# A decoder block in one program: the stream that prepares the feed-forward operands, its steps, its engines and the order behind it

## The chip, the core and the metric

One core of a Trainium2 chip runs the whole kernel as one program. The metric is the device time of one execution in microseconds (us), the median of several runs. A profiled execution of the same program gives, for each engine, when each instruction ran. The engines are TensorE (PE, with weight loads as PEld), VectorE (DVE), ScalarE (ACT), GpSimd (POOL) and SyncE (SP), which here only issues DMAs. Each engine works through its own queue in order; semaphores tie the queues together. SBUF is the on-chip memory of 128 partitions, PSUM the memory that PE writes, and the DRAM tensors lie in HBM.

## What is computed

One decoder layer on a sequence of 2048 tokens of width 1024, in float32. A mixer sub-layer (windowed attention beside an mLSTM, gated and merged, then `w_out`) gives `x`, and a SwiGLU feed-forward network (FFN) of width 2816 follows:

```python
x = x + gate_m[:, None, :] * rms_norm(mix, g_post_mix[l])

h2 = modulate(rms_norm(x, g_pre_ffn[l]), shift_f, scale_f)
ff = (jax.nn.silu(h2 @ w_ffn_gate[l]) * (h2 @ w_ffn_up[l])) @ w_ffn_down[l]
x = x + gate_f[:, None, :] * rms_norm(ff, g_post_ffn[l])
```

The change concerns `h2`, the first operand of the FFN's matmuls.

## The kernel before, in words

**Tiles and numbers.** Every float32 matmul is done as three matmuls of split numbers: a value is cut into a high part (ACT copies it to the reduced format, `split_unit`, L1112) and a low part (DVE subtracts, L1113), and high x high, high x low and low x high are added up in PSUM. Each such matmul has 512 columns.

**Mixer.** Four blocks of 512 tokens (`block(b)`) run one after the other. A block ends with the mLSTM's branch projection (`branch_tiles` on `w_bm`, 96 matmuls) and the output projection with the residual (`residual_out`, 2 halves of 96 matmuls). The residual's tail, for each of four token tiles: ACT squares the sum (L523), DVE multiplies by the gain (L525), POOL raises to the power -1/2 (L473), DVE and POOL add to rows of `x` that were loaded by L552 (L537, L540), SP writes the new `x1` (L541), ACT squares again (L542), DVE adds the sums (L543), and POOL makes `rx`, the reciprocal norm for the next sub-layer. These use the buffers `tx` (6 of them); most other scratch of the mixer is `tm` (9).

**FFN.** Tokens are taken in two halves of 1024 (`b2`). For each half, `gate_up(b2)` makes gate and up projections and `down(b2)` the down projection. Each product of 2x2 blocks is done with seven block products instead of eight (a Winograd-Strassen form). The seven right operands are called, in the order of the products, 11, 21, T2, T4, T1, T3, 22 (`PROD`); 11, 12, 21, 22 are the quarters of the transposed `h2` and the T's are differences of them. The seven left operands are quarters of the weights and their sums: 11, 12, S2, 22, S1, S3, S4. S1 and S2 are made by DVE (L1254, L1255) into buffers `w` that `unit()` takes from the FFN's pool.

**The stream that is changed.** `h_combine(b2, ...)` makes the right operands, in four steps `k` (a quarter of the width's 128-column groups each). A step loads four pieces of `x1` by four DMAs (L1193), multiplies each by `rx` (L1197), transposes them on PE (L1204, L209) into PSUM, scales and shifts them to 11, 12, 21, 22 (ACT L1209, DVE L1207), makes T1, T2, T3, T4 by subtractions (L1214 to L1222), and splits all seven. For the first half of tokens it runs inside the last mixer block: its pieces lie in `tm` buffers, its products and differences are done by POOL (`G` in `HC_FROM_MIXER`), and since SBUF is full at that point, two operands are **parked**: T3 and 22 are written to the DRAM tensor `hc_d` (L1224) and read back by `rest_of_hc` (L1237), which makes their low parts (L1240) and 22's high part (L1239) once the mixer's buffers are given up. For the second half it runs inside `down(0)`, all on DVE, with pieces in `big` buffers.

**What sets the order.** The kernel is written out by Python in one pass. PE's work is written as it comes, and a planned clock `now` is advanced by each matmul. Streams are generators: `yield d` means "go on when `now` has advanced by `d` ns". `spawn(gen, delay)` starts one, `tick()` steps those that are due, and `finish` steps a stream to its end whatever the clock says. In the mixer `tick` runs after each group of matmuls. In `run2`, which drives the FFN, it runs only in parts marked `weave`, that is, in those of the seven down products that accumulate into one PSUM group (first, third, fifth and seventh, 11 parts each). The written order is the priority; when the program is built, each engine's queue is laid down from it by what is then expected to be ready.

`run2` itself loads weights ahead and prepares up to four parts (gate and up) or two (down) ahead: this is `advance()`, called before and after each part. Between mixer and FFN stands `open_ffn`: it closes the mixer's pools, opens the FFN's pool over the same memory (each tile waits for those it overlays), loads the gain `gg_f` there (L1497), and calls `rest_of_hc`. The FFN's first `advance()` came after that.

Of the kernel before, what the change touches and what calls it, by code (L numbers as in the profile page):

```python
# [19 lines left out]
P = 128  # L20
# [47 lines left out]
def decoder_block(ctx: ExitStack, tc: tile.TileContext, a: dict, out: bass.AP, dbg=None):  # L68
# [582 lines left out]
    def block(b):  # L651
# [393 lines left out]
        def stage5():  # L1045
            finish(R["ml"])
            finish(R["outs"])
            if b + 1 == NBLK:
                finish(R_ada)
                open_hc()  # L1050
                R["hc"] = spawn(h_combine(0, *HC_FROM_MIXER), 8000.0)
            for i in range(2):
                A.activation(R["gm", i], R["gm", i], AF.Sigmoid)

# [67 lines left out]
    def run2(items):  # L1122
        items = list(items)
        parts = [p for p in items if isinstance(p, Part)]
        raws = []
        for p in parts:
            if p.raw not in raws:
                raws.append(p.raw)
        nload = nprep = done = 0
        made = {}  # L1130

        def advance():
            nonlocal nload, nprep
            while True:
                alive = sum(1 for r in raws[max(0, nload - 3):nload] if r.left)
                if nload < len(raws) and alive < 2:
                    raws[nload].tile = raws[nload].load()
                    nload += 1
                    continue
                if nprep < len(parts) and nprep < done + parts[nprep].ahead and parts[nprep].raw.tile is not None:  # L1140
                    p = parts[nprep]
                    made[nprep] = p.prep()
                    p.raw.left -= 1
                    nprep += 1
                    continue
                return

        for it in items:
            if not isinstance(it, Part):
                it()  # L1150
                continue
            advance()
            for _ in it.mms(made.pop(done)):
                if it.weave:
                    tick()
            done += 1
            advance()
# [21 lines left out]
    def four(t):  # L1179
        return [t[:, i * 4:(i + 1) * 4, :] for i in range(4)]  # L1180


    HC_FROM_MIXER = (lambda: [tm([P, 4, P]) for _ in range(4)], lambda: tm([P, TB]), lambda: tm([P, TB]), G)

    def h_combine(b2, rows, quarters, sums, eng):


        wait = b2 == 0
        for k in range(4):
            xk = rows()  # L1190
            for j, (half, i) in enumerate(((0, 0), (0, 1), (1, 0), (1, 1))):
                c0 = (k + 4 * half) * P
                nc.sync.dma_start(xk[j], x1[b2 * 2 + i][:, c0:c0 + P].rearrange("(t p) c -> p t c", p=P))  # L1193
            yield 12000.0
            for j in range(4):
                t0 = b2 * 8 + (j % 2) * 4
                eng.tensor_tensor(xk[j], xk[j], rx[:, t0:t0 + 4].unsqueeze(2).to_broadcast([P, 4, P]), op=ALU.mult)  # L1197
            yield 4000.0
            v = {}
            for j, (half, i) in enumerate(((0, 0), (0, 1), (1, 0), (1, 1))):  # L1200
                kk = k + 4 * half
                ps = mix_tile()
                for t in range(4):
                    transpose(ps[:, t * P:(t + 1) * P], xk[j][:, t, :])  # L1204
                q = quarters()
                if wait and i:
                    V.tensor_scalar(q, ps, s2[:, kk:kk + 1], sh2[:, kk:kk + 1], op0=ALU.mult, op1=ALU.add)  # L1207
                else:
                    A.activation(q, ps, AF.Identity, scale=s2[:, kk:kk + 1], bias=sh2[:, kk:kk + 1])  # L1209
                v[f"{half + 1}{i + 1}"] = q  # L1210
                if i:
                    yield 1500.0
            v["T1"] = sums()
            eng.tensor_tensor(v["T1"], v["12"], v["11"], op=ALU.subtract)  # L1214
            v["T2"] = sums()
            eng.tensor_tensor(v["T2"], v["22"], v["T1"], op=ALU.subtract)
            eng.tensor_tensor(v["12"], v["22"], v["12"], op=ALU.subtract)
            v["T3"] = v.pop("12")
            for name in NAMES:
                if name == "T4":  # L1220
                    v["T4"] = sums()
                    eng.tensor_tensor(v["T4"], v["21"], v["T2"], op=ALU.subtract)  # L1222
                if wait and name in ("T3", "22"):
                    nc.sync.dma_start(hc_d[:, ("T3", "22").index(name), k, :], v[name])  # L1224
# [8 lines left out]
    def rest_of_hc():  # L1233
        for i, name in enumerate(("T3", "22")):
            for k in range(4):
                u = unit()
                nc.sync.dma_start(u, hc_d[:, i, k, :])  # L1237
                if name == "22":
                    A.copy(hc_part("22", 0)[:, k, :], u)  # L1239
                V.tensor_tensor(hc_part(name, 1)[:, k, :], u, HC[name][0][:, k, :].bitcast(F32), op=ALU.subtract)  # L1240
# [158 lines left out]
    def down(b2):  # L1399
# [71 lines left out]
        if not last:  # L1471
            def next_h():
                q4 = []

                def quarters():
                    if not q4:
                        t = big([4, TB])
                        q4.extend(t[:, i, :] for i in range(4))
                    return q4.pop()

                F["hp"] = spawn(h_combine(b2 + 1, lambda: four(big([16, P])), quarters, unit, V))

            yield next_h
        for i in range(7):
# [8 lines left out]
    def open_ffn():  # L1493
        p1.close()
        F["pool"] = ctx.enter_context(tc.tile_pool(name="fpool", bufs=1, reuse_waits="tile"))
        F["gg"] = F["pool"].tile([P, D], F32, name="gg_f")
        nc.sync.dma_start(F["gg"], gg_f_d)  # L1497
        rest_of_hc()

    def program():  # L1500
        for i, ch in enumerate(ADA):
# [7 lines left out]
    open_ffn()  # L1509

    def program2():
        for b2 in range(NB2):
            yield from gate_up(b2)
            yield from down(b2)
# [28 lines left out]
```

## Time and profile before

| | us |
|---|---|
| median of 3 runs | 2827.76 |
| lowest and highest run | 2825.27, 2830.12 |
| the profiled execution, its own time | 2826.42 |
| its span, first to last instruction | 2824.6 |

The page of the profile lists the busy time of each engine, the span in 40 slices, and the costliest groups of instructions. A row of a timeline has start, duration, engine, line, operation, what it writes and reads (buffer numbers left out), its shape and a count when neighbours are merged; in brackets stands the idle time of the engine just before it and who ended it. Rows with SPq are DMA issues. A view by form gives minimum, median and maximum duration in ns and the first and last start. A matmul is in flight longer than the next one waits, so the cost of one is the distance from start to start.

### The profile page before, as it was taken

Reading aid. Unit: us, or ns where it says so; the run is one execution under the profiler, and the core shown is the slowest. Engines: PE = TensorE matmul, PEld = TensorE weight load, DVE = VectorE, ACT = ScalarE, POOL = GpSimd, SP = SyncE. Lnnn points to the kernel's source line nnn. Section 1 sums busy time; section 2 is a strip of 40 time slices with the busy share of each in tenths; the row PEclk is TensorE's granted clock in tenths of the full one; section 3 lists DMA queues with packets and bytes.
Section 4 is the critical chain, followed back from the end, with each engine's and each line's share of the span. In section 5 each row is a group of like instructions: output and inputs, shape, how many; then the busy total and the mean of one; then the engine's idle time right before and its main releaser. Section 6 shows DMA issues by size and latency. Waiting matters only on the chain.

```text
span 2824.6 us, 35115 instructions
## 1 busy us (share of the span) xinstructions
PE 2720.0 (96%) x12654; PEld 2204.8 (78%) x12654; DVE 1935.0 (69%) x3756; ACT 1226.6 (43%) x2269; POOL 283.2 (10%) x287
## 2 busy tenths in 40 slices
PE   6999999999999999999987999999998999999997
PEld 4778887788877887778876788887776888888886
DVE  7768666586575876757677966766757666666556
ACT  4543365434644336543343333334554333333443
POOL 3100120012200012101272000000000000000000
PEclk8999999999999999999998999999999999999999
DMA  7234252243522425323357932335557233234557
GB/s 228 90 108 106 95 188 93 82 116 107 181 87 82 133 81 182 100 81 97 94 182 244 308 109 97 112 110 170 194 179 241 95 112 105 97 108 140 181 197 242
DMA packets 274773, 392.14 MB, mean 139 GB/s; under 512 B 18580, under 2 KB 175896, under 8 KB 274600
## 3 DMA queue, kind: packets, MB, share of 16 engines
q1 hardware_dynamic: 274600, 389.91, 43.0%
q8 instruction: 99, 1.62, 0.2%
q14 instruction: 74, 0.61, 0.1%
HBM read 318.52 MB, written 71.34 MB: 138 GB/s over the span
## 4 chain that ended last, share of the span: by engine, by line
PE 81%; DVE 8%; DMA 7%; ACT 2%; issue 1%; POOL 1%; SPq 0%; DVEq 0%; POOLq 0%; ACTq 0%
PE acc L204 57%; PE mix L204 22%; PE mix L209 2%; DVE hl L1113 1%; DMA tx<-in_x_dram 1%; DMA big<-in_w_ffn_down_dram 1%; DMA ws_d<-big 1%; DMA tx<-in_w_ada_dram 1%; DVE tm L424 1%; DMA raw<-in_w_ffn_down_dram 1%; ACT hl L1112 1%; DMA x<-tx 0%; DMA raw<-as_d 0%; DVE wlo L260 0%; DMA big<-in_x_dram 0%
## 5 line engine op out<-in xcount | busy, mean ns | idle before, releaser
L1112 ACT CAST hl<-raw 128x512 fp32r<-128x512 f32 x528 | 314.7, 621 | 444.3 <-PE mix L204 189.4
L1113 DVE TENSOR_TENSOR hl<-raw,hl 128x512 fp32r<-128x512 f32 x528 | 352.5, 688 | 191.0 <-ACT hl L1112 188.8
L259 ACT CAST whi<-raw 128x1024 fp32r<-128x1024 f32 (+1 forms) x208 | 212.1, 1020 | 476.0 <-PE acc L204 417.5
L260 DVE TENSOR_TENSOR wlo<-raw,whi 128x1024 fp32r<-128x1024 f32 (+1 forms) x208 | 255.4, 1228 | 173.1 <-ACT whi L259 172.1
L204 PE MATMUL acc<-hhi,wlo 128*128 128x512 f32 x896 | 354.5, 396 | 0.0
L204 PE MATMUL acc<-hlo,whi 128*128 128x512 f32 x896 | 352.1, 393 | 0.0
L204 PE MATMUL acc<-hhi,whi 128*128 128x512 f32 x896 | 352.0, 393 | 0.0
L204 PE MATMUL acc<-hl,hl 128*128 128x512 f32 x1056 | 252.4, 397 | 18.4 <-DVE hl L1113 12.1
L204 PE MATMUL acc<-big,hl 128*128 128x512 f32 x1056 | 253.7, 389 | 0.0
L204 PEld LDWEIGHTS acc<-hl,hl 128*128 128x128 f32 x1056 | 198.0, 190 | 68.6 <-DVE hl L1113 18.7
L204 PEld LDWEIGHTS acc<-big,hl 128*128 128x128 f32 x1056 | 198.2, 188 | 41.2
L204 PEld LDWEIGHTS acc<-hlo,whi 128*128 128x128 f32 x896 | 168.3, 188 | 41.0 <-issue 6.5
L204 PEld LDWEIGHTS acc<-hhi,whi 128*128 128x128 f32 x896 | 168.4, 188 | 39.5 <-issue 6.5
L204 PE MATMUL mix<-big,hl 128*128 128x512 f32 x704 | 197.4, 391 | 1.4 <-DVE hl L1113 1.4
L204 PEld LDWEIGHTS acc<-hhi,wlo 128*128 128x128 f32 x896 | 168.3, 188 | 38.5 <-issue 4.1
L204 PE MATMUL mix<-hl,hl 128*128 128x512 f32 x792 | 182.1, 390 | 1.3 <-ACT hl L1112 1.2
L204 PEld LDWEIGHTS mix<-hl,hl 128*128 128x128 f32 x792 | 148.0, 188 | 34.9 <-ACT hl L1112 4.2
L473 POOL TENSOR_TENSOR rs<-ms,nhalf 128x1 f32<-128x1 f32 (+1 forms) x40 | 29.2, 733 | 1436.0 <-DVE ms L470 1409.7
L204 PE MATMUL acc<-whi,big 128*128 128x512 f32 x512 | 165.9, 396 | 0.0
L204 PE MATMUL acc<-big,whi 128*128 128x512 f32 x512 | 157.9, 393 | 0.0
L204 PEld LDWEIGHTS mix<-big,hl 128*128 128x128 f32 x704 | 132.2, 188 | 30.3 <-DVE hl L1113 2.2
L204 PE MATMUL acc<-wlo,hhi 128*128 128x512 f32 (+1 forms) x384 | 139.7, 368 | 3.3 <-DVE wlo L260 2.5
(317 smaller groups left out, 5014.6 us busy)
## 6 DMA issues: line engine op xcount, KB each, us to landing
raw<-in_w_in_dram SPq DMA_DIRECT2D x76, 1024.0 KB, 5.4
as_d<-w SPq DMA_DIRECT2D x154, 256.0 KB, 2.1
raw<-as_d SPq DMA_DIRECT2D x70, 512.0 KB, 3.8
raw<-in_w_ffn_gate_dram SPq DMA_DIRECT2D x22, 1024.0 KB, 6.8
raw<-in_w_ffn_up_dram SPq DMA_DIRECT2D x22, 1024.0 KB, 5.4
raw<-ws_d SPq DMA_DIRECT2D x40, 512.0 KB, 4.7
tx<-in_w_ada_dram SPq DMA_DIRECT2D x64, 256.0 KB, 4.2
raw<-in_w_out_dram SPq DMA_DIRECT2D x16, 1024.0 KB, 5.0
```

What stands on the lines that cost most here:

```text
L204: T.matmul(o, lhsT=lhsT, rhs=rhs, start=start, stop=stop, skip_group_check=resumed)
L209: T.transpose(o, i, ident[:k, :k])
L259: A.copy(hv, src)
L260: eng.tensor_tensor(lv, src, hv.bitcast(F32), op=ALU.subtract)
L424: V.scalar_tensor_tensor(acc, raw[:, k, :], c_, acc, op0=ALU.mult, op1=ALU.add)
L473: G.tensor_tensor(r[:, :n], ms[:, :n], nhalf[:, :n], op=ALU.pow)
L1112: A.copy(v(hi), src)
L1113: V.tensor_tensor(v(lo), src, v(hi).bitcast(F32), op=ALU.subtract)
```

## The change

Four things change.

1. `h_combine` for the first half starts 3000 ns of planned time after its spawn (before: 8000), its first rows are followed by 8000 (before: 12000 in each step), and the products by 3000 (before: 4000). The rows of step `k + 1` are loaded inside step `k`, after its transposes and ahead of its differences.
2. The one engine becomes a pair. The first stream gets (POOL, DVE): products alternate, T1 and T2 go to POOL, T3 and T4 to DVE. The second stream gets (DVE, DVE). T1, T2 and T4 of the first stream now lie in `tx` buffers, before in `tm`.
3. `run2` calls `advance()` once before it looks at its first item.
4. `rest_of_hc` is no longer called in `open_ffn`, but is the first item of the FFN's program, so it is written after that first `advance()`.

The steps of `h_combine` are the same for the second half, so its spacing changes too.

```diff
-                R["hc"] = spawn(h_combine(0, *HC_FROM_MIXER), 8000.0)
+                R["hc"] = spawn(h_combine(0, *HC_FROM_MIXER), 3000.0)
...
+        advance()
         for it in items:
             if not isinstance(it, Part):
                 it()
...
-    HC_FROM_MIXER = (lambda: [tm([P, 4, P]) for _ in range(4)], lambda: tm([P, TB]), lambda: tm([P, TB]), G)
+    HC_FROM_MIXER = (lambda: [tm([P, 4, P]) for _ in range(4)], lambda: tm([P, TB]), lambda: tx([P, TB]), (G, V))
 
-    def h_combine(b2, rows, quarters, sums, eng):
+    def h_combine(b2, rows, quarters, sums, engs):
 
         wait = b2 == 0
-        for k in range(4):
+        QUADS = ((0, 0), (0, 1), (1, 0), (1, 1))
+
+        def load(k):
             xk = rows()
-            for j, (half, i) in enumerate(((0, 0), (0, 1), (1, 0), (1, 1))):
+            for j, (half, i) in enumerate(QUADS):
                 c0 = (k + 4 * half) * P
                 nc.sync.dma_start(xk[j], x1[b2 * 2 + i][:, c0:c0 + P].rearrange("(t p) c -> p t c", p=P))
-            yield 12000.0
+            return xk
+
+        xn = load(0)
+        yield 8000.0
+        for k in range(4):
+            xk = xn
             for j in range(4):
                 t0 = b2 * 8 + (j % 2) * 4
-                eng.tensor_tensor(xk[j], xk[j], rx[:, t0:t0 + 4].unsqueeze(2).to_broadcast([P, 4, P]), op=ALU.mult)
-            yield 4000.0
+                engs[j % 2].tensor_tensor(xk[j], xk[j], rx[:, t0:t0 + 4].unsqueeze(2).to_broadcast([P, 4, P]), op=ALU.mult)
+            yield 3000.0
...
                 if i:
                     yield 1500.0
+            if k < 3:
+                xn = load(k + 1)
             v["T1"] = sums()
-            eng.tensor_tensor(v["T1"], v["12"], v["11"], op=ALU.subtract)
+            engs[0].tensor_tensor(v["T1"], v["12"], v["11"], op=ALU.subtract)
             v["T2"] = sums()
-            eng.tensor_tensor(v["T2"], v["22"], v["T1"], op=ALU.subtract)
-            eng.tensor_tensor(v["12"], v["22"], v["12"], op=ALU.subtract)
+            engs[0].tensor_tensor(v["T2"], v["22"], v["T1"], op=ALU.subtract)
+            engs[1].tensor_tensor(v["12"], v["22"], v["12"], op=ALU.subtract)
             v["T3"] = v.pop("12")
...
-                    eng.tensor_tensor(v["T4"], v["21"], v["T2"], op=ALU.subtract)
+                    engs[1].tensor_tensor(v["T4"], v["21"], v["T2"], op=ALU.subtract)
...
-                F["hp"] = spawn(h_combine(b2 + 1, lambda: four(big([16, P])), quarters, unit, V))
+                F["hp"] = spawn(h_combine(b2 + 1, lambda: four(big([16, P])), quarters, unit, (V, V)))
...
-        rest_of_hc()
...
     def program2():
+        yield rest_of_hc
         for b2 in range(NB2):
```

More of the change, by code (lines that the diff above doesn't have):

```diff
@@ L1180, in four @@
         return [t[:, i * 4:(i + 1) * 4, :] for i in range(4)]
-    HC_FROM_MIXER = (lambda: [tm([P, 4, P]) for _ in range(4)], lambda: tm([P, TB]), lambda: tm([P, TB]), G)
-    def h_combine(b2, rows, quarters, sums, eng):
+    HC_FROM_MIXER = (lambda: [tm([P, 4, P]) for _ in range(4)], lambda: tm([P, TB]), lambda: tx([P, TB]), (G, V))
+    def h_combine(b2, rows, quarters, sums, engs):
         wait = b2 == 0
-        for k in range(4):
+        QUADS = ((0, 0), (0, 1), (1, 0), (1, 1))
+        def load(k):
             xk = rows()
-            for j, (half, i) in enumerate(((0, 0), (0, 1), (1, 0), (1, 1))):
+            for j, (half, i) in enumerate(QUADS):
                 c0 = (k + 4 * half) * P
                 nc.sync.dma_start(xk[j], x1[b2 * 2 + i][:, c0:c0 + P].rearrange("(t p) c -> p t c", p=P))
-            yield 12000.0
+            return xk
[3 more added lines that the diff above has]
+            xk = xn
             for j in range(4):
                 t0 = b2 * 8 + (j % 2) * 4
-                eng.tensor_tensor(xk[j], xk[j], rx[:, t0:t0 + 4].unsqueeze(2).to_broadcast([P, 4, P]), op=ALU.mult)
-            yield 4000.0
+                engs[j % 2].tensor_tensor(xk[j], xk[j], rx[:, t0:t0 + 4].unsqueeze(2).to_broadcast([P, 4, P]), op=ALU.mult)
+            yield 3000.0
             v = {}
-            for j, (half, i) in enumerate(((0, 0), (0, 1), (1, 0), (1, 1))):
+            for j, (half, i) in enumerate(QUADS):
                 kk = k + 4 * half
```

## The prediction

> **What bounds the kernel now.** I read the page first, then the busy time by windows, the table of waits of the matmul engine, and the timelines of each engine around the one hole.
>
> ```profile
> span 2824.6 us, 35115 instructions
> PE 2720.0 (96%) x12654; PEld 2204.8 (78%) x12654; DVE 1935.0 (69%) x3756; ACT 1226.6 (43%) x2269; POOL 283.2 (10%) x287
> PE   6999999999999999999987999999998999999997
> POOL 3100120012200012101272000000000000000000
> ```
>
> PE is the bound, so an edit pays only where PE stands still. Slices 21 and 22 of the 40 are such a place, and there POOL is at its busiest. By windows (us, then busy of PE, PEld, DVE, ACT and POOL, the granted clock, the DMA share and GB/s):
>
> ```profile
> 1440.00:1460.00 20.00, 20.00 (x98) 16.70 (x97) 14.61 (x15) 10.47 (x20) 10.26 (x7) 1.00 0.59 184
> 1460.00:1480.00 20.00, 12.62 (x62) 9.71 (x60) 15.66 (x21) 11.77 (x27) 13.09 (x12) 0.85 0.68 228
> 1480.00:1500.00 20.00, 9.63 (x31) 7.03 (x31) 14.51 (x21) 10.44 (x21) 17.14 (x15) 0.59 0.45 154
> 1500.00:1520.00 20.00, 13.98 (x49) 10.72 (x50) 17.19 (x29) 7.14 (x13) 0.00 (x0) 0.71 0.80 276
> ```
>
> This is the passage from the last mixer block to the FFN. PE's timeline shows where it stands:
>
> ```profile
> 1444.56 1.36 PE L209 MATMUL mix<-ident,tm 128*128 128x128 f32 x11
> 1469.76 1.63 PE L204 MATMUL acc<-hc,hl 128*128 128x512 f32 x6
> 1481.41 1.12 PE L209 MATMUL mix<-ident,tm 128*128 128x128 f32 x4 [7.43 <-POOL tm L1197]
> 1506.02 0.80 PE L204 MATMUL acc<-hcT2h,hl 128*128 128x512 f32 x1 [13.35 <-ACT hl L1112]
> 2098.99 30.50 PE L204 MATMUL mix<-hl,hl 128*128 128x512 f32 x132 [1.17 <-ACT hl L1112]
> ```
>
> A matmul of 512 columns costs 30.50 / 132 = 0.231 us, a transpose 1.36 / 11 = 0.12 us. The FFN's first product starts at 1469.76. Then PE waits for the stream's last quarter of rows (7.43 us) and for the weight operand S2 of the third product (13.35 us). From 1469.76 to 1506.02 it does 24 matmuls (two products) and the 16 transposes of that quarter: 5.5 + 1.9 = 7.4 us of work in 36.3. So 28.9 us are lost, and no edit of this passage can give more.
>
> **Why the wait for S2 ends at 1506.02.** From the timelines of DVE, ACT and SP:
>
> ```profile
> 1464.97 0.60 ACT L523 ACTIVATE tx<-acc 128x512 f32<-128x512 f32 x1 [1.27 <-PE acc L204]
> 1497.75 0.16 DVE L543 TENSOR_TENSOR sx<-sx 128x1 f32<-128x1 f32 x1
> 1497.93 0.32 SPq L1497 DMA_DIRECT2D gg_f<-gg_f_d  x1
> 1498.34 4.09 SPq L1237 DMA_DIRECT2D w<-hc_d  x8
> 1502.81 0.69 DVE L1240 TENSOR_TENSOR big<-w,big 128x512 fp32r<-128x512 f32 x1 [4.71 <-DMA w<-hc_d]
> 1503.42 0.68 DVE L1254 TENSOR_TENSOR w<-raw 128x512 f32<-128x512 f32 x1
> 1507.03 0.69 DVE L1240 TENSOR_TENSOR big<-w,big 128x512 fp32r<-128x512 f32 x1
> 1513.05 0.69 DVE L1240 TENSOR_TENSOR big<-w,big 128x512 fp32r<-128x512 f32 x1
> ```
>
> S1 and S2 live in the FFN's pool, which lies on the mixer's tx and tm buffers. Everything of that pool stands behind the mixer's tail: 1464.97, the first evacuation of the last half, to 1497.75, the last sum of squares, is 32.8 us. Behind the tail DVE first waits 4.71 us for a parked operand (L1240, read back from hc_d), and only then makes S1 (L1254). S1's start to PE's start is 1506.02 - 1503.42 = 2.6 us.
>
> **The change, step by step. Delays.** A quarter of the stream takes 12 + 4 + 1.5 + 1.5 + 1.5 = 20.5 us of planned PE time, four and the start 90. What follows on PE is 96 + 192 = 288 matmuls, 288 x 0.231 = 66.5 us. So the last quarter falls out behind them, as seen. With the edit it is 3 + 8 + 4 x 7.5 = 41 us, so the whole stream lies under matmuls. Its transposes are not saved, only moved: the mixer's end, and with it the first evacuation, comes 1.9 us later, at 1466.9.
>
> **The tail.** Three earlier blocks have the same tail without this stream, but with other streams in it (adaLN weights in tx, the next block's rows). Block 0:
>
> ```profile
> 396.25 0.60 ACT L523 ACTIVATE tx<-acc 128x512 f32<-128x512 f32 x1 [0.90 <-PE acc L204]
> 402.06 0.16 DVE L543 TENSOR_TENSOR sx<-sx 128x1 f32<-128x1 f32 x1 [0.17 <-ACT big L542]
> 406.52 0.15 DVE L543 TENSOR_TENSOR sx<-sx 128x1 f32<-128x1 f32 x1
> 419.13 0.15 DVE L543 TENSOR_TENSOR sx<-sx 128x1 f32<-128x1 f32 x1
> ```
>
> That is 22.9 us from end to end. If all four token tiles followed at the pace of the first two, 5.8 + 3 x 4.5 = 19.2. So the tail is between 19.2 and 32.8 us; I take 22, near block 0 but with less beside it. It ends at 1466.9 + 22 = 1488.9.
>
> **Weights first.** S1 now precedes the parked operands, so the 4.7 us go; with S1 0.2 us behind the tail and 2.4 us of chain (one L1240 less between), the third product starts at 1491.5 instead of 1506.0: **14.5 us gained**. What is late next is the parked operands. Their loads still stand in SP's queue behind gg_f and hence behind the tail: T3's fourth piece ends 1507.03 + 0.69 - 1497.75 = 10.0 us after the tail, the last of "22" 16.0 us after it. PE needs T3 36 matmuls after the third product, 2.6 + 8.3 = 10.9, and "22" at 13.7. So "22" may come up to 2.3 us late; I take 1.5, nothing if DVE gets to it sooner.
>
> **Work shared.** Durations and the loads' latency, from the views by form of L1197 and L1193:
>
> ```profile
> L1197 POOL TENSOR_TENSOR tm<-tm,rx x16: 1040/1488/2019, 1385.8 to 1485.2; 128x512 f32<-128x512 f32 x16
> L1197 DVE TENSOR_TENSOR big<-big,rx x16: 683/690/694, 1614.8 to 2020.1; 128x512 f32<-128x512 f32 x16
> L1193 SPq DMA_DIRECT2D tm<-x x16: 359/466/1373, 1379.5 to 1477.9; - x16
> DMA to landing us min/median/max: 3.0/4.0/4.8
> ```
>
> Per quarter POOL gives up 4 of 8 operations (about 4 x 1.49 = 6 us), DVE takes 4 x 0.69 = 2.8 us, 11 us in all. DVE is 14.61 of 20 us busy in the window above and weight pieces are split two ahead, so I cost this at nothing; uncovered it is 11 us. The sums now sit in tx, beside the residual's buffers; the stream should be over before the last half needs them.
>
> **Rows loaded earlier, closer steps.** Rows of the next quarter reuse the four tm buffers just transposed, so they can't start before those transposes. Load to ready is 4 x 0.47 issue + 4.0 landing + two POOL products 3.0 = 8.9 us, and the kernel plans 4.5 us from load to transposes. The order of PE's queue is laid down at build time; if it trusts that plan, PE waits up to 4.4 us in each of three quarters, 13.2 us. Below, it is nothing: before, PE waited for no transpose ahead of the last quarter. I take 0.5 us for each, 1.5.
>
> The Trainium skill bears on the sharing: "SBUF — State Buffer", section "Who interferes with whom", says that a DVE instruction with two SBUF inputs and a GpSimd instruction that reads SBUF lock each other out for a whole instruction. The rows agree:
>
> ```profile
> 1433.92 1.53 DVE L1113 TENSOR_TENSOR big<-tm,hcT4h 128x512 fp32r<-128x512 f32 x1
> 1433.04 6.74 POOL L1197 TENSOR_TENSOR tm<-tm,rx 128x512 f32<-128x512 f32 x4
> ```
>
> Beside POOL that DVE subtraction takes 1.53 us, while DVE's products without POOL take 0.69. By the rule two and two products follow one another and 4.4 us becomes 4.4 + 1.4 = 5.8; by overlap it stays 4.4.
>
> **The second stream** runs under the first down projection, on DVE alone, with the same new spacing:
>
> ```profile
> 1920.97 1.03 PE L209 MATMUL mix<-ident,big 128*128 128x128 f32 x8
> 1994.68 0.60 PE L209 MATMUL mix<-ident,big 128*128 128x128 f32 x4
> 2009.86 0.63 PE L209 MATMUL mix<-ident,big 128*128 128x128 f32 x4 [0.39 <-DVE big L1197]
> 2020.26 10.05 PE L204 MATMUL acc<-hl,hl 128*128 128x512 f32 x36 [3.53 <-DVE hl L1113]
> 1920.00:1940.00 20.00, 18.12 (x86) 14.35 (x86) 14.54 (x24) 10.08 (x17) 0.00 (x0) 1.00 0.56 164
> 2000.00:2020.00 20.00, 15.67 (x74) 12.04 (x72) 19.24 (x33) 15.65 (x28) 0.00 (x0) 1.00 0.78 248
> ```
>
> It is stepped only in the products that weave, 132 matmuls or 30.5 us at a time. Before, one quarter falls in the first weave and two in the next, where DVE is full (19.24 of 20) and PE loses 4.3 us; with the first weave's 1.9 that is 6.2. With 7.5 us per quarter three fall in the first. A quarter costs DVE 15 x 0.69 = 10.4 us (four products, four differences, seven splits), the eleven parts 22 x 0.69 = 15.2. That is 46 us in 30.5; less the lead of two parts (5.5) it is 10 us lost in place of 6.2. So between -6.2 (no loss) and +10; I take +2.
>
> **Sum.** 14.5 - 1.5 - 1.5 - 2 = 9.5 us off the profiled execution's own 2826.42 us (span 2824.6 and 1.8 around it): 2816.9. That execution lies 1.3 us under the median of the three runs, 2827.76; I forecast **2817**.
>
> **Rivals.** *Clean:* tail at 19.2, no new waits: 14.5 + 2.8 = 17.3, so 2809. For it: POOL, which served the tail's powers late, is nearly free then. Against: DVE's backlog at the FFN's start.
>
> *No change:* the tail doesn't shorten, since its buffers turn over by DMA and not by POOL (it keeps 32.8 us and ends at 1499.7; the third product starts at 1502.3, 3.7 us earlier, and the other terms take 5.0), or the transposes of the first stream wait in full (14.5 less 1.5, 13.2 and 2). That gives 2828 and 2829. The first is also the case that the change doesn't do what it says: PE would only wait elsewhere. The three blocks at 23 us speak against it.
>
> *Slower:* one mechanism, transposes ordered ahead of their rows, in both streams: six quarters x 4.4 = 26.4 us against 14.5 - 1.5, so 2840. It decides from 13 / 6 = 2.2 us a quarter on. For it: planned 4.5 us against 8.9. Against: the second stream's waits are 0.39 us at most, and a list that knows the products to be unready would put matmuls first.
>
> **Chances.** Forecast (2811 to 2821) 0.42, clean 0.25, no change 0.17, slower 0.16. A measurement of this kernel tells about 0.2% from no change, 5.7 us. Faster by more: 0.67; within: 0.17; slower: 0.16. The range goes from 2804, some us under the clean case for a second stream without loss, to 2832, with part of the slower case left out. The likeliest case's own range is 2811 to 2821.
>
> **What would show it.** After the change POOL's products end before the last half's first evacuation, and no transpose stands behind the mixer's last matmul. The tail (first L523 to last L543 of the last block) is 19 to 24 us. DVE makes S1 before the first L1240. PE still has one hole of about 12 us ahead of the third product. If PE's waits name L1197 during the mixer, the spacing was too tight; if they name L1113 near the down projection's start, DVE is what the second stream lacks. If the tail keeps 33 us, I misread what holds it.

## The result, and the profile after

The changed kernel takes 2835.57 us, the median of 14 runs, against 2824.69 us for the kernel before in the same comparison: ratio 1.0038, 95% interval 1.0029 to 1.0047. It is **slower by 0.38%**, 10.9 us, where 2817 was forecast. The profiled execution took 2836.65 us.

The page of the kernel after, its span, two of its engines and POOL's 40 slices:

```profile
span 2834.9 us, 35116 instructions
PE 2726.6 (96%) x12654; PEld 2210.2 (78%) x12654; DVE 1933.0 (68%) x3772; ACT 1225.6 (43%) x2269; POOL 259.7 (9%) x271
POOL 3100121012200112101241000000000000000000
```

POOL is relieved in slice 21 (4 tenths, before 7), as meant. The same stretches of the passage by windows (us, then busy of PE, PEld, DVE, ACT, POOL, granted clock, DMA share, GB/s), and the first of them in the kernel before:

```profile
1420.00:1440.00 20.00, 18.10 (x86) 14.14 (x84) 20.00 (x21) 10.61 (x17) 14.51 (x8) 1.00 0.57 165
1440.00:1460.00 20.00, 16.08 (x75) 12.82 (x76) 18.55 (x21) 11.08 (x16) 9.54 (x7) 0.89 0.55 166
1460.00:1480.00 20.00, 12.37 (x45) 9.75 (x44) 11.46 (x15) 6.41 (x15) 3.70 (x2) 0.68 0.25 79
```
```profile
1420.00:1440.00 20.00, 20.00 (x94) 16.55 (x93) 15.41 (x13) 8.53 (x12) 18.37 (x11) 1.00 0.44 132
```

PE was busy for 20.00 of 20 us in the first two windows before. Now DVE is full (20.00) and PE stands inside the mixer. In the kernel after, L1205 are the stream's products, L1224 and L1226 (POOL) its sums T1 and T2, L1264 is S1, L1250 the low parts of the parked operands; `wlo` (L260) is the low part of the mixer's weights. PE's table of waits from 1385 to 1500, and its timeline (the last row is the product that was third to start, 22 by T4):

```profile
PE acc L204 <- DVE big L525: 7.6, 1, 7.6
PE acc L204 <- DVE wlo L260: 2.3, 1, 2.3
PE mix L209 <- POOL tm L1205: 2.1, 2, 1.3
PE mix L209 <- DVE tm L1205: 1.4, 2, 0.9
```

```profile
1441.25 0.50 PE L204 MATMUL acc<-wlo,big 128*128 128x512 f32 x1 [2.27 <-DVE wlo L260]
1468.18 0.80 PE L204 MATMUL acc<-whi,big 128*128 128x512 f32 x1 [7.63 <-DVE big L525]
1492.28 2.65 PE L204 MATMUL mix<-hc,hl 128*128 128x512 f32 x11
1510.35 0.80 PE L204 MATMUL mix<-hcT4h,hl 128*128 128x512 f32 x1 [12.47 <-ACT hl L1112]
```

The FFN's first product starts at 1492.28, before at 1469.76. The longest new wait is for L525, the evacuation of the residual's *first* half: PE can't begin the second half while all four accumulators are full. L525 reads the same accumulators behind the squares of L523 on ACT. The timelines of ACT, POOL and DVE show why both are late:

```profile
1462.93 0.62 ACT L1112 CAST big<-tx 128x512 fp32r<-128x512 f32 x1 [2.15 <-POOL tx L1224]
1464.60 0.62 ACT L1112 CAST hcT2h<-tx 128x512 fp32r<-128x512 f32 x1 [1.05 <-POOL tx L1226]
1465.12 0.59 ACT L523 ACTIVATE tx<-acc 128x512 f32<-128x512 f32 x1
1489.08 0.60 ACT L523 ACTIVATE tx<-acc 128x512 f32<-128x512 f32 x1 [1.12 <-PE acc L204]
1460.79 2.11 POOL L1224 TENSOR_TENSOR tx<-tm,tm 128x512 f32<-128x512 f32 x1 [2.62 <-ACT hc L1112]
1467.44 2.47 DVE L525 TENSOR_TENSOR big<-acc,gg_m 128x512 f32<-128x512 f32 x4
1507.45 0.16 DVE L543 TENSOR_TENSOR sx<-sx 128x1 f32<-128x1 f32 x1 [2.10 <-ACT big L542]
1507.72 0.68 DVE L1264 TENSOR_TENSOR w<-raw 128x512 f32<-128x512 f32 x1
1513.33 0.69 DVE L1250 TENSOR_TENSOR big<-w,big 128x512 fp32r<-128x512 f32 x1 [1.19 <-DMA w<-hc_d]
```

The squares stand in ACT's queue behind splits of the stream's last sums, which wait for POOL. The row at 1465.12 has no bracket: nothing it needs is late, only its queue. L525 has none either: by then it stands in DVE's queue behind the stream's last sums and splits. In the kernel before, ACT's timeline has these squares at 1441.34:

```profile
1441.34 0.60 ACT L523 ACTIVATE tx<-acc 128x512 f32<-128x512 f32 x1 [1.34 <-PE acc L204]
```

(The Trainium skill, "Perfetto Trace Analysis", section "Tensor Engine Instruction (MATMUL, LD_WEIGHTS)", says that ACT, DVE and GpSimd keep strict order; the trace agrees.) The last three rows of the view after show the forecast parts that did come: the tail is 1507.45 - 1489.08 = 18.4 us (before 32.8), and S1 (L1264) follows at once, ahead of the parked operands (L1250).

Then the FFN's start. A view of the early sums of the down weights, and rows of DVE and PE:

```profile
L1354 DVE TENSOR_TENSOR big<-big x11: 684/693/694, 1520.6 to 1622.5; 128x512 f32<-128x512 f32 x11
  DMA big<-in_w_ffn_down_dram: 9.1, 4
  issue: 8.5, 3
```
```profile
1560.01 0.69 DVE L1354 TENSOR_TENSOR big<-big 128x512 f32<-128x512 f32 x1 [5.47 <-issue]
1563.76 3.59 PE L204 MATMUL mix<-big,hl 128*128 128x512 f32 x10 [2.93 <-DVE hl L1113]
```

For each of 11 pieces of the down weights DVE makes four sums, which only the down projection needs: they are first read back at 2014.8. They are written one piece for every fourteen products, but in the built queue all eleven lie between 1520 and 1623. DVE waits there for their rows (9.1 us), and the splits for the next product stand behind. Another 8.5 us the view puts down to nobody ("issue"); the row at 1560.01 is one of these, and its rows were late too: the load was issued at 1553.53, and these loads take 6.2 us to land. PE's waits from 1500 to 1680, other than the one at 1510.35, all name the low parts of splits (L1113, 9.5 us).

**The account.** I use one measure for all kernels. Count the matmuls of 512 columns from the first evacuation of the last half. *Lost* at the n-th is its start less that evacuation, less n x 0.2272 us, about the spacing of matmuls back to back (0.227); for the second stream's stretch, from the 1800th to the 2900th, I also take off 0.12 us for each transpose. The *hole*, PE's wait ahead of the third product, lies in the first 60. *Mixer late* is the shift of that evacuation against 1464.97, less the shift that was there upstream, before the first stream starts. Each row is one profiled execution, which can lie some us off its kernel's median (e16: 2816.71 against 2809.32; e15: 2795.70 against 2801.12).

| kernel (difference) | ratio to before, 95% | mixer late | lost by 60th | 60th to 650th | 1800th to 2900th |
|---|---|---|---|---|---|
| before | | 0 | 35.4 | 6.0 | 28.7 |
| after | 1.0038 (1.0029-1.0047) | 22.8 | 14.5 | 15.1 | 28.6 |
| e1 order edit alone | 0.9986 (0.9974-0.9998) | 0.0 | 29.4 | 9.3 | 21.5 |
| e2 after, old order | 1.0039 (1.0025-1.0052) | 22.1 | 20.3 | 6.8 | 26.1 |
| e3 squares elsewhere | 1.0000 (0.9989-1.0011) | 14.0 | 16.7 | 9.2 | 28.0 |
| e6 sums in tm | 0.9994 (0.9983-1.0004) | 13.6 | 17.0 | 9.1 | 26.0 |
| e7 e6, POOL alone | 1.0004 (0.9994-1.0013) | 16.0 | 17.4 | 9.1 | 29.2 |
| e8 e6, w buffers | 0.9968 (0.9956-0.9980) | 13.7 | 17.1 | 0 | 28.6 |
| e9 e6, old second stream | 0.9982 (0.9973-0.9992) | 13.7 | 16.7 | 6.2 | 25.0 |
| e10 e6, wider steps | 0.9984 (0.9976-0.9993) | 11.3 | 15.9 | 7.6 | 29.4 |
| e11 e1, w buffers | 0.9949 (0.9935-0.9964) | 0.0 | 29.3 | 0 | 23.8 |
| e12 e8 + e9 + e10 | 0.9940 (0.9929-0.9952) | 11.2 | 15.8 | 0.2 | 26.0 |
| e13 before, w buffers | 0.9971 (0.9960-0.9981) | 0.0 | 35.9 | 0 | 28.5 |
| e14 e12, 22 split first | 0.9922 (0.9909-0.9935) | 11.2 | 14.4 | 0.2 | 19.4 |
| e15 e14, DVE alone | 0.9921 (0.9908-0.9933) | 3.6 | 15.7 | 0.2 | 20.5 |
| e16 e11, 22 split first | 0.9954 (0.9941-0.9967) | 0.0 | 30.1 | 0 | 28.2 |
| e17 e14, still wider | 0.9936 (0.9923-0.9948) | 11.2 | 16.4 | 1.1 | 22.3 |
| e18 e6, DVE alone | 0.9998 (0.9985-1.0010) | 8.2 | 15.6 | 12.0 | 28.6 |

Before to after: 1.3 us upstream, +22.8 in the mixer, -20.9 in the hole, +9.1 at the FFN's start, -0.1 in the second stream, -1.9 in the last products: +10.3, as the spans differ.

### The profile page after: what moved, and what is told of

It reads as the page before. It is cut to its first block, busy times and chain, and to the rows that moved or that the text cites. A ratio compares the mean times of both kernels' runs of the same rounds, so it can differ in the third digit from the quotient of the medians.

```text
span 2834.9 us, 35116 instructions
## 1 busy us (share of the span) xinstructions
PE 2726.6 (96%) x12654; PEld 2210.2 (78%) x12654; DVE 1933.0 (68%) x3772; ACT 1225.6 (43%) x2269; POOL 259.7 (9%) x271
## 5 line engine op out<-in xcount | busy, mean ns | idle before, releaser
L1113 DVE TENSOR_TENSOR hl<-raw,hl 128x512 fp32r<-128x512 f32 x528 | 352.4, 689 | 194.2 <-ACT hl L1112 191.8
L260 DVE TENSOR_TENSOR wlo<-raw,whi 128x1024 fp32r<-128x1024 f32 (+1 forms) x208 | 251.5, 1210 | 179.5 <-ACT whi L259 178.4
```

Of the source, the lines that this page charges most:

```text
L260: eng.tensor_tensor(lv, src, hv.bitcast(F32), op=ALU.subtract)
L1113: V.tensor_tensor(v(lo), src, v(hi).bitcast(F32), op=ALU.subtract)
```

## The experiments

Theory when they began: the sums T1, T2, T4 take turns with the residual's scratch in `tx`, and buffers of one tag are handed out in the order in which the code is written. The stream's sums now come ahead of the first half's squares. Rivals: the steps are too close whatever the buffer; the shared work fills DVE; the order edit costs the FFN's start.

### The two halves of the change

**e1**, the kernel before with parts 3 and 4 alone:

```diff
+        advance()
         for it in items:
...
-        rest_of_hc()
...
+        yield rest_of_hc
```

> The kernel before with the order behind the stream alone changed (the first loading-ahead of the FFN's parts ahead of the read-back of the parked operands); stream, spacing, engines and buffers are those of before. Theory (the loss of 20.6 us at the mixer's end comes from the stream's new written place and buffers, the order edit only lets S1 go first): the mixer's end stays at 1469.8 +- 1.5 us, the tail keeps about 32.8 us and ends near 1497.8, S1 follows at once, the third product starts at 1500 to 1502.5 in place of 1506.0; then 0 to 6 us are given back where DVE's queue is held by the early sums of the down weights: total ratio 0.998 to 1.001. Rival A (the order edit alone costs the 6 us at the FFN's start): the ratio is above 1.000, and the drift against before grows by 6 us between 1520 and 1640. Rival B (the order edit gains nothing, since S1 also waits for the tail's buffers): the third product within 1 us of 1506.

2819.38 us. The mixer's end stays, the third product comes 6.0 us of lost time earlier and 3.3 of it are given back by the 650th, as the theory had it; in the profiled execution the second stream's stretch, where nothing was changed, also lost 7.2 us less, and the ratio came out at the better end.

**e2**, the kernel after with those lines taken back.

> The kernel after without the order edit (read-back of the parked operands ahead of the first loading-ahead, as before); the stream is that of after. Theory: the mixer's end is as late as in after (first FFN product at 1492 +- 1.5), S1 stands behind the first read-back again, so the third product comes about 4 to 5 us later than in after (1514 to 1516 in place of 1510.4). Rival (the 6 us lost at the FFN's start come from the order edit): those come back, so the whole is 2 us faster than after or the same; without that rival it is 4 to 5 us slower than after, ratio 1.005 to 1.006.

2834.11 us, the same as after. The order edit is worth 5.8 us at the hole (20.3 to 14.5) and costs 8.3 behind it (6.8 to 15.1). So in the changed kernel it gained nothing, and the rival was right that something behind S1 takes it back. What that is, e8 shows.

### The sums in tx

**e3** takes the squares out of `tx`, **e6** the sums:

```diff
-            junk = tx([P, 512])
+            junk = st["keep"][:, t, :] if hf == 0 else tx([P, 512])
```
```diff
-    HC_FROM_MIXER = (lambda: [tm([P, 4, P]) for _ in range(4)], lambda: tm([P, TB]), lambda: tx([P, TB]), (G, V))
+    HC_FROM_MIXER = (lambda: [tm([P, 4, P]) for _ in range(4)], lambda: tm([P, TB]), lambda: tm([P, TB]), (G, V))
```

> The kernel after, but the squares of the last residual's first half (of every block) are written to the place where the normed half is kept, in place of a tx buffer; nothing else. Theory (tx buffers are handed out in written order, and three sums of each quarter now take their turn among them, so the first half's evacuation stands behind the last quarter of the stream): the first half's squares run at 1443 to 1450 again in place of 1465, the wait of 7.6 us of PE for DVE's evacuation goes, the first FFN product starts at 1478 to 1484 in place of 1492.3, and the whole is 8 to 13 us faster than after: ratio to before 0.999 to 1.001. Rival spacing (the last quarter collides in the queues with the evacuation whatever the buffer): the squares stay at 1460 or later, the first FFN product within 3 us of 1492, the ratio stays 1.003 to 1.005. Rival engines (DVE full with the shared products): the wait moves, first FFN product 1488 to 1492.

> The kernel after with the sums T1, T2, T4 of the first stream in tm buffers, as before; spacing, engines and order are those of after. Theory tx: as with the squares elsewhere, the first half's squares run at 1443 to 1450, PE's wait of 7.6 us goes and the first FFN product starts at 1478 to 1484; but the sums now take turns with the pieces of x1 in tm, so the next quarter's loads wait for the splits of this one's sums: 0 to 6 us more. Ratio to before 0.998 to 1.002. Rival spacing: squares at 1460 or later, ratio 1.003 to 1.005. Rival engines: as after within 3 us.

2823.58 and 2822.23 us. First squares of e3, ACT's timeline, then of e6:

```profile
1453.66 0.59 ACT L523 ACTIVATE big<-acc 128x512 f32<-128x512 f32 x1
```
```profile
1452.71 0.59 ACT L523 ACTIVATE tx<-acc 128x512 f32<-128x512 f32 x1
```

Either way PE's wait of 7.6 us is gone, and the mixer's end comes 8.8 and 9.2 us earlier. Two different edits, each taking one member out of the tie, give the same: **the tie in tx is shown**, at about 9 us of the 22.8. The squares are still 11 to 12 us later than in the kernel before; the theory had expected them back at 1443 to 1450. About 13.6 us of lateness remain.

### The rest of the late mixer

**e7** is e6 with `(G, G)`, **e10** e6 with `yield 6000.0` in place of 3000 for the first stream.

> The kernel with the sums in tm (the run before this one that undid the tx part) with one thing more undone: products and differences of the first stream all on POOL again. That kernel still ends its mixer 13.5 us later than the kernel before (first evacuation of the last half at 1478.4 against 1465.0, 0.2 us of it from upstream), 1.9 us of it transposes moved ahead, and its DVE was busy 5.00 of 5.00 us from 1420 to 1450. Theory engines (the shared work fills DVE, where the weight pieces' low parts then come late): the 4.2 us wait for wlo and the half clock behind it go, the first evacuation of the last half comes at 1468 to 1474, ratio to before 0.996 to 0.998. Rival spacing (7.5 us per quarter is less than load, products and transposes need, whoever does them): POOL alone is slower, PE waits for POOL's products at L209 in three quarters, 3 to 5 us each, first evacuation at 1478 to 1486, ratio 0.999 to 1.004.

> The kernel with the sums in tm, and in the first stream 6000 in place of 3000 between products and transposes: 10.5 us of planned time per quarter, 53 us in all, and 7.5 us planned from a load to its transposes. Theory spacing (the stream's work per quarter does not fit in 7.5 us; what stays of the late mixer end is PE waiting for rows and weights while DVE is full): DVE drops under 4.7 of 5 us between 1420 and 1450, the wait of 4.2 us for wlo goes, the first evacuation of the last half comes at 1468 to 1473, but the last sums stand closer to the tail; ratio to before 0.995 to 0.998. Rival (it is the amount of work and not its spacing): as with the sums in tm within 2 us. Second rival (the last quarter now collides with the last half's tail): first evacuation early but the tail longer than 21 us, S1 at 1497 or later.

2825.88 and 2820.01 us. POOL alone is no better: PE waits 2.4 us for wlo (4.2 in e6), but 5.4 for POOL's products. Wider steps give 2.3 us, less than that run's theory had. Neither finds the other 11 us. What both kept is POOL working beside DVE. **e15** is the frame of e14 (below) with the stream on DVE alone, **e17** the same frame with 9000, **e18** is e6 on DVE alone:

```diff
-    HC_FROM_MIXER = (..., lambda: tm([P, TB]), (G, V))
+    HC_FROM_MIXER = (..., lambda: tm([P, TB]), (V, V))
```

> The fastest kernel so far (all together, 22 split ahead of S2) with products and differences of the first stream all on DVE. Theory lock (DVE instructions with two SBUF inputs run 1.5 to 1.8 us beside POOL in place of 0.69, 8.8 us in all between 1400 and 1478; rows from the kernel with all together): 16 POOL operations go, DVE gets 16 x 0.69 = 11 us more and loses most of the 8.8, while each step of the stream is ready 1 us earlier: the wait for wlo falls from 3.4 to under 2, the first evacuation of the last half comes 2 to 5 us earlier than 1476.8, total 2797 to 2801. Rival (DVE has too much work, whatever its pace): DVE 5.00 of 5 us from 1420 to 1455, waits for wlo of 5 us or more, first evacuation at 1479 to 1484, total 2805 to 2810.

> The fastest kernel so far with 9000 in place of 6000 between products and transposes of the first stream: 13.5 us per quarter, 65 us in all, so that the last quarter falls into the last half's matmuls. Theory spacing: waits for wlo 3.4 to under 1.5 us, first evacuation of the last half at 1472 to 1475 in place of 1476.8, but T4's last pieces are ready later and the tail is longer by 0 to 4 us; total 2798 to 2803. Rival (spacing has given what it has): the same within 2 us, or slower by the tail.

2801.12 us for e15, 2806.82 for e17, whose mixer is as late as that of e14: wider steps have given what they had. Windows of e15:

```profile
1420.00:1440.00 20.00, 20.00 (x98) 16.53 (x97) 19.92 (x28) 10.97 (x17) 3.98 (x2) 1.00 0.52 161
1440.00:1460.00 20.00, 20.00 (x106) 16.77 (x105) 20.00 (x31) 14.11 (x26) 0.00 (x0) 1.00 0.59 195
```

DVE is as full as in the kernel after, yet it does 28 and 31 instructions in these windows in place of 21 and 21, and PE is busy throughout. From 1400 to the mixer's end, e14 first, then e15:

```profile
1400.00:1476.80 76.80, 72.44 (x335) 58.43 (x334) 65.38 (x75) 40.31 (x62) 33.74 (x22) 0.98 0.48 158
```
```profile
1400.00:1467.82 67.82, 67.82 (x329) 56.26 (x328) 63.33 (x89) 39.77 (x62) 12.54 (x8) 1.00 0.52 164
```

DVE runs 89 instructions in 63.3 us; in e14 it ran 75 in 65.4. More work takes no more time, because the instructions that were long in e14 are shorter. T3's subtraction in both, by form from 1400 to the mixer's end (count, busy us and mean ns), e14 first:

```profile
L1231 DVE TENSOR_TENSOR tm<-tm,tm 128x512 f32<-128x512 f32 x4 | 6.6, 1648 | 0.0
```
```profile
L1231 DVE TENSOR_TENSOR tm<-tm,tm 128x512 f32<-128x512 f32 x4 | 2.7, 677 | 0.0
```

It is made by DVE in both kernels. DVE's instructions that read an accumulator and one SBUF tile (L1061) took 690 ns on average in both, though in e14 the one at 1405.81 ran in the middle of a POOL instruction (1405.52 to 1406.81). The mixer is 3.6 us late, about what the 31 transposes moved ahead cost at 0.12. (This is the Trainium skill's rule in "SBUF — State Buffer", section "Who interferes with whom", that the prediction weighed for 1.4 us of row products. The trace agrees with it, and its price was on many of DVE's instructions with two SBUF inputs, not on the row products alone.) The edit also makes the stream's own operations shorter, since they leave the slower POOL; but in e14 PE's waits in the mixer name `wlo` (3.4 us) and L525 (0.9), both of DVE, and none names POOL. In total e14 and e15 can't be told apart (2802.52 and 2801.12); the gain of 7.6 us in the mixer is read from the two traces, of which 1.3 go back by the 60th matmul. The same edit on e6 (e18, next) takes 5.4 us off the mixer.

> The kernel after with one line changed: the first stream's sums in tm and all its products and differences on DVE. Theory (these two are what made the mixer's end late; the run with DVE alone ended its mixer 3.6 us late, just the 3.7 us of the transposes moved ahead, with no wait of PE in the mixer): first evacuation of the last half at 1468 to 1471 in place of 1489.1, the tail as in the kernel after, so the third product at 1490 to 1495, as the forecast had it (1491.5); the 9 us of the early sums stay; total 2810 to 2816, ratio to before 0.995 to 0.997. Rival (the wider steps were needed too: at 7.5 us per quarter DVE has more than it can do): first evacuation at 1474 to 1480, total 2818 to 2823.

2822.82 us, where the theory had 2810 to 2816; the rival, that the wider steps are needed too, is nearer. The mixer is 8.2 us late (forecast 3 to 6; at close steps PE still waits 2.5 us for DVE's products at L209), the third product starts at 1496.66, and the stretch of the early sums then loses 12.0 us. PE's and DVE's timelines of e18:

```profile
1496.66 0.80 PE L204 MATMUL mix<-hcT4h,hl 128*128 128x512 f32 x1 [13.70 <-ACT hl L1112]
1606.90 0.69 DVE L1354 TENSOR_TENSOR big<-big 128x512 f32<-128x512 f32 x1 [3.18 <-DMA big<-in_w_ffn_down_dram]
```

### What takes back the gain behind the hole

The 650th matmul starts at 1654.0 in the kernel before, 1653.5 in e1, 1654.4 in e3, 1652.1 in e6 and 1649.4 in e18, though their third products start between 1496.7 and 1506.0. **e8** (on e6), **e11** (on e1) and **e13** (on the kernel before) load the pieces into `w` buffers, which turn over with the products:

```diff
-            st["raw"] = big([2, D])
-            nc.sync.dma_start(st["raw"], wdn[p * 256:(p + 1) * 256, :].rearrange("(k p) c -> p k c", p=P))
+            for k in range(2):
+                for h in range(2):
+                    st[k, h] = unit()
+                    nc.sync.dma_start(st[k, h], wdn[p * 256 + k * P:p * 256 + (k + 1) * P, h * TB:(h + 1) * TB])
...
```

> The kernel with the sums in tm, and the rows of the down weights from which sums are made loaded into four w buffers a piece (four DMAs in place of one, into buffers that turn over with the FFN's products) in place of a big buffer. In all kernels so far the eleven pieces' sums run bunched together at 1514 to 1622 (written order spreads them over 430 us), with the DMA share at 0.85 to 0.98 there and PE losing 9 us to late operands between the 60th and the 650th product matmul behind the mixer's end (6.0 in the kernel before). Theory burst (these sums block DVE's queue while their rows are late): the sums spread out beyond 1700, those 9 us become 0 to 4, and the whole is 4 to 9 us faster than with the sums in tm alone, ratio to before 0.996 to 0.998. Rival (DVE is short of time there with or without them, from the parked operands and the split of weights): still 7 to 10 us lost, and no gain. Second rival: the w buffers, 16 in all, run short and PE waits elsewhere along the 430 us: slower than with the sums in tm by 3 us or more.

> The kernel with the order edit alone, and the down weights' rows in w buffers. With the order edit alone the third product of the FFN starts 5.9 us of lost time earlier (29.4 in place of 35.4 us lost at the 60th product matmul behind the mixer's end), but from there to the 650th it loses 9.3 where the kernel before loses 6.0. Theory burst (the early sums hold DVE's queue, and whoever comes earlier meets more of it): 9.3 become 0 to 1, 29 to 30 us lost at the 650th; ratio to before 0.995 to 0.997, 5 to 7 us better than the control (the kernel before with the same edit). Rival (the order edit costs those 3 us by itself, through the parked operands that now stand behind): 3 us or more stay lost between the 60th and the 650th, and it is 2 to 3 us better than the control.

> The control: the kernel before with one edit, the down weights' rows in w buffers. Theory burst: the 6.0 us that it loses between the 60th and the 650th product matmul become 0 to 1, the hole ahead of the third product stays as it is (35.4 lost); ratio to before 0.997 to 0.999. Rival (in the kernel before the parked operands alone cost those 6 us): no difference, ratio 0.999 to 1.001.

2815.07, 2810.14 and 2817.17 us. The sums in e8, and PE's whole table of waits from 1500 to 1680:

```profile
L1356 DVE TENSOR_TENSOR w<-w,w x11: 679/692/694, 1517.8 to 1897.2; 128x512 f32<-128x512 f32 x11
```
```profile
PE mix L204 <- ACT hl L1112: 13.8, 1, 13.8
```

Spread over 380 us, the sums cost nothing: in all three kernels the loss behind the 60th matmul is gone. The order edit with them is worth 7.0 us between e13 and e11 (medians) and 6.6 at the 60th matmul. So **the order edit gained what it should, and the bunched sums took part of it**: shown on e1 and e6. The edit spreads the loads of the rows as well as the sums, so these runs don't tell DVE's queue from the crowded loads (DMA share from 1540 to 1560: 0.89 in the kernel after, 0.59 in e8); that PE's waits name L1113 speaks for the queue. On the kernel after itself the w buffers were not tried; why it loses 15.1 where e3 and e6 lose 9 stays open.

### The second stream, and all together

**e9** is e6 with the second stream's old steps (load at the head, 12000, 4000); **e12** joins e8, e9 and e10; **e14** adds, for the first part, the split of 22 ahead of that of S2; **e16** is e11 with that.

```diff
                     if name == "S2":
+                        if first:
+                            st["22"] = split_unit(q(1, 1))
                         t = st["S2"]
...
```

> The kernel with the sums in tm, and for the second stream alone the steps of the kernel before (rows loaded at the head of each step, 12000 and 4000 in place of 3000). Between the 1800th and the 2900th product matmul behind the mixer's end the kernel before lost 28.7 us against back-to-back matmuls, the kernel after 28.5, the one with sums in tm 26.0: with the new steps 8 to 10 us fall in the first woven product (three quarters of the stream in 31 us) in place of 0.6, and less later. Theory (the two balance, the size of the later part is chance of order): 21 to 29 us lost, 0.6 to 1 of them in the first woven product, ratio to before 0.998 to 1.001. Rival (the old steps are worth the 7 us by which the run with the order edit alone fell in this stretch, 21.5): 21 to 22 us lost, ratio 0.997 to 0.998.

> All that helped, together: the kernel after with the sums in tm, 6000 in place of 3000 in the first stream, the second stream's steps as before, the down weights' rows in w buffers. If the terms add up: 2815.1 with the w buffers, less 2.2 for the spacing, less 0 to 3 for the second stream: 2810 to 2813, ratio to before 0.995 to 0.996. If the gains of the steps apart lay in the same stretch (the early sums), no more than with the w buffers alone: 2815. It also tells whether the shared stream is worth anything: if the run with the order edit and w buffers alone is as fast, the stream's loading ahead and its shared work bring nothing.

> All together, and for the first part of the FFN the left operand 22 (a plain quarter of the weights) is split ahead of S2. In the runs so far PE stands 13.7 us ahead of the third product, which is 22 by T4: its operands need nothing of the tail, but 22's split stands in ACT's queue behind S2's, which waits for DVE's sums in buffers that the tail gives up. Theory (a queue in order holds work that is ready): the 12 matmuls of 22 by T4 move into the hole, the wait becomes 10 to 11 us and names ACT or DVE for S2, 2.7 us faster than all together: ratio 0.994 to 0.995. Rival (the split tiles are not free earlier, or T4's low part is late): the same hole, the same time within 1 us.

> The stream of the kernel before (POOL alone, late start, 20.5 us per quarter, sums in tm) in the frame of the fastest kernel: order edit, w buffers for the down weights, 22 split ahead of S2. With the two edits without the last it ran 2810.1 where the new stream ran 2808.7 (intervals of 4 us). Theory (the new stream is worth nothing: what the tail gains, the mixer's end gives back): 2803 to 2809; here the last quarter's transposes stand ahead of T4, so the split of 22 gains less than the 6 us that it gained there: 0 to 3. Rival (the new stream lets 22 by T4 move into the hole and the old can't): 2808 to 2812, 6 to 9 us slower than with the new stream.

2819.20, 2808.65, 2802.52 and 2809.32 us. With old steps the first woven product (1900th to 2000th matmul) loses 0.6 us, with new ones 7.8 (e6) and 9.1 (after); later parts lose less in turn, so the stretch as a whole hardly moves (25.0 against 26.0). In e14 the product 22 by T4 follows the second one directly, and the hole stands behind it; PE's timeline:

```profile
1485.44 0.39 PE L204 MATMUL mix<-hcT4h,hl 128*128 128x512 f32 x1
1499.81 0.80 PE L204 MATMUL mix<-big,hl 128*128 128x512 f32 x1 [11.48 <-ACT hl L1112]
```

That explains 1.4 us of the 6 that e14 gains on e12 (lost at the 650th, 14.6 against 16.0). Most of the rest lies in the second stream's stretch (19.4 against 26.0), where the two kernels are written alike; the stretch moved between 19.4 and 29.4 us through all runs, and by what is not settled. For the same reason e16's 2809.32 says little on the stream. Mixer and 650th matmul together do: the new stream shared (e12) stands at 27.2 and the old one (e11) at 29.2; with 22 split first the new one stands at 25.8 shared (e14) and 19.5 on DVE alone (e15), the old one (e16) at 30.1. The split of 22 gains nothing in e16, as PE waits 6.3 us for T4's own high part there.

## Why the prediction was wrong, point by point

- **"The sums now sit in tx ... the stream should be over before the last half needs them": the step that failed first.** I asked who else uses tx at the tail, not who uses it at the first half. In planned time the last sums are written at 3 + 8 + 3 x 7.5 + 6 = 39.5 us. The first half is evacuated behind 96 + 96 matmuls, which the kernel's planned clock counts at 0.216 us each (L203), so at 41.5 or later, and its squares come behind the sums. Cost: 9 us, shown by e3 and e6.
- **"Work shared ... I cost this at nothing": the second.** I added DVE's new instructions at 0.69 us to a window with 5 us free. With POOL beside it some of them, and some that DVE had already, take far longer (T3 1.44 us on average in the kernel after, 1.65 in e14). Less the transposes, 9.9 us of the 13.6 are left for this and for the close steps: e15 ends its mixer 7.6 us earlier than e14, e18 5.4 earlier than e6, e10 2.3 earlier than e6. I weighed the rule for the row products alone. My uncovered price of 11 us was near by luck: it stood for added work, not for slower instructions, and I took zero.
- **Transposes:** 1.9 forecast for one quarter; 31 were moved, two quarters, 3.7 us.
- **The tail:** 22 forecast, 18.4 measured, below my lower end of 19.2. Right in direction.
- **Weights first:** right. S1 starts 0.27 us behind the tail, the third product 2.6 behind S1. From the mixer's end the hole lost 20.9 us less; the forecast's 14.5 and 1.9 make 16.4. The start at 1491.5 failed only because the mixer ended late.
- **The FFN's start:** absent from my sum. I named DVE's backlog there against the clean case and gave it no price; it took 9.1 us. This is the term that also stops e1 and e18.
- **Rows loaded earlier:** 1.5 taken, 3.5 measured at L209, inside its bounds.
- **The second stream:** +2 taken, -0.1 measured. The loss of 10 us in the first weave is there (9.1, before 0.6), and so is its return later.
- **The rivals:** the slower one gave 2840, near the result by luck: its mechanism was 26.4 us of transposes waiting in both streams, and they waited 3.5 us in the first and 0.5 in the second.

## What to carry to other kernels

Before moving work to an idle-looking engine or a free-looking buffer, list all users of that tag and that queue in written order, the ones upstream too, and ask what the engine beside it does to each of its instructions. Time gained ahead of a stretch where queues hold work needed much later is taken back there; pace such work by buffers that turn over with the products, which here was worth 8 us even to the kernel before. The two best kernels, e14 and e15, take 0.9922 and 0.9921 of the time before.

## What the runs showed of the hardware

DVE did 14 instructions more in 2 us less once the stream's work was off POOL, whose busy time in the stretch fell from 33.7 to 12.5 us (e14 to e15). Behind PE's wait of 7.6 us in the kernel after, matmuls ran 0.43 us apart in place of 0.227, at a granted clock that the windows of the kernel after show as 0.50:

```profile
1465.00:1470.00 5.00, 1.82 (x4) 1.49 (x5) 5.00 (x10) 3.56 (x11) 0.00 (x0) 0.50 0.63 229
```

About ten matmuls ran so, some 2 us more (10 x 0.2). This hole cost more than its length.
